# Spreading a recurrence's output projection over three attention stages, in a decoder layer on one core

## The chip, the cores and the metric

The kernel runs on one core of a Trainium2 chip. A core has a matrix engine (TensorE, PE in the profile), a vector engine (DVE), a scalar engine (ACT), a general engine (POOL), and a queue processor that issues transfers (SP); POOL issues transfers too. Each engine takes its instructions in a fixed order and waits on semaphores. The metric is the device time of one execution in microseconds (us), the median of several runs.

## The reference

One layer of a hybrid decoder on 2048 prompt tokens and 8 sample tokens of width 1024. The prompt attends to 256 chosen keys for each query, by softmax over 8 heads; a gated recurrence makes the other half of the mixer's width; one output projection, a residual, RMSNorm and an MLP of width 4096 follow.

```python
aq = rms_norm(aq.reshape(B, L, ATT_HEADS, ATT_HEAD_DIM), q_norm_g)
...
logits = jnp.einsum('btkgd,btskd->btkgs', qg, k_sel).astype(jnp.float32) * ATT_SCALE
logits = jnp.where(valid[:, :, None, None, :], logits, -jnp.inf)
p = jax.nn.softmax(logits, axis=-1).astype(v_sel.dtype)
...
x = x + jnp.concatenate([att, rec.astype(att.dtype)], axis=-1) @ w_out
h2 = rms_norm(x, norm2_g)
x = x + jnp.square(jax.nn.relu(h2 @ w_up)) @ w_down
```

## The kernel before

All products are made in 32-bit precision as three products of a high and a low part (`mm3`, L127 to L129: high by high, high by low, low by high). Rows are tiles of 128 tokens, 16 of the prompt and one with the 8 sample tokens.

The first 1059 us hold the input projection, the indexer, the recurrence and the first choices of keys. From there the rows go through in three groups of tiles (`GROUPS`: 0 to 4, 5 to 10, 11 to 16), each with three stages: attention (`attend_all`), output projection with the second norm (the first loop of `mlp_group`), MLP (its second loop). In attention a unit is one pair of heads of one tile, four units to a tile: `logits` (products `lg`, L993; mask and running maximum on DVE, L995, tile `mx`; the maximum times minus the scale, L1001, tile `nm`; the exponential on ACT, L1002), then `values` (transposes `pt`, L1016; high part on ACT, `ph`; low part on DVE, `pl`; products into `O`, L1031 and L1032, or L1029 in the first five tiles; last two transposes `ob`, L1039). The logits of a unit are issued between the values of the unit before.

The recurrence's half of the output projection does not need the attention: `recurrence_out` makes it for all 16 tiles inside the first group's attention. For a tile it loads the recurrence's rows (`rt`, L929) and the residual (`y`, L931, one buffer), makes four transposes, 24 products of 512 columns into `po`, two additions on DVE (L945), and stores `y` to DRAM (`yD`). `mlp_group` loads `yD` later and adds the attention's half to it (64 additions of 256 columns, L1698).

A tile scheduler sets the order on each engine: it places instructions by priority and by a simulated timeline, in program order for equal priority. Side work is fed in by hand: `along` goes through the steps of a stage, counts the columns that PE processes, and takes one step of a `Track` whenever its rate in columns is reached. Beside the first MLP run the choice of keys for tiles 8 to 11 (`choosing`, 12000 columns a step) and the sample's first part (7000); beside the second MLP run the choice for tiles 12 to 15 (14000) and the sample's second part (9000), which begins with a search by counts over rows of 1025 on DVE (L1333). All start with the output projection of their group.

Weights are loaded in pieces of 512 KB (`load_cols`, `load_row`), rounded to a high part on ACT (L1570); the low part is made on POOL at the first use and reloaded from DRAM afterwards.

## Time and profile before

| | |
|---|---|
| runs before: median (lowest to highest) | 3517.41 us (3514.81 to 3519.64) |
| the profiled execution: its own time | 3515.95 us |
| the profiled execution: span of its instructions | 3514.2 us |
| mean granted TensorE clock, as a share of full speed | 0.977 |
| PE, DVE, ACT, POOL busy, share of the span | 94%, 67%, 63%, 34% |

The busy time of PE counts a product from its start to its modelled end, and products overlap, so that a share of 94% does not mean 94% of what PE could do. Shares over the span hide that the stages differ; the rows further down are taken stage by stage.

### The profile page before, as it was taken

The numbers are of one execution on the slowest core, as the hardware profiler recorded it, in microseconds if no ns is written. First come the engines' busy times: TensorE is split into PE (matmuls) and PEld (weight loads), VectorE is DVE, ScalarE is ACT, GpSimd is POOL, SyncE is SP. The second block draws the span as 40 slices with busy tenths as digits, with TensorE's granted clock in tenths as the row PEclk, the third lists the DMA queues.
The fourth block names the chain that finished last, engine by engine and source line by source line (L and its number), as shares of the span: only waits on it lengthen the run. The fifth ranks groups of instructions, "written<-read, shape, count | busy, mean of one in ns | idle before, by whom it ended". The sixth has DMA issues, their size and how long they took to land. (4 is left out here: it accounts for less than half of the span.)

```text
span 3514.2 us, 56706 instructions
## 1 busy us (share of the span) xinstructions
PE 3315.7 (94%) x20230; PEld 2912.1 (83%) x20230; DVE 2345.8 (67%) x5150; ACT 2202.5 (63%) x4063; POOL 1201.2 (34%) x1460
## 2 busy tenths in 40 slices
PE   8999889999998989989999988999999999999999
PEld 7787788999996778877787778888989788888888
DVE  3577788877684358898795788796384787322323
ACT  5789887777674258858844665765973576333332
POOL 5565776655544035554442101042211000100000
PEclk9999999999999999999999999999999999999999
DMA  6564647464535446555546112334336201444443
GB/s 212 156 177 146 176 144 194 139 165 133 163 104 192 146 133 209 190 170 167 168 148 223 36 59 88 126 100 163 130 127 226 84 25 37 150 144 141 135 136 129
DMA packets 343244, 499.95 MB, mean 142 GB/s; under 512 B 38536, under 2 KB 252144, under 8 KB 341936
## 3 DMA queue, kind: packets, MB, share of 16 engines
q1 hardware_dynamic: 280784, 326.35, 29.4%
q0 software_dynamic: 62176, 169.96, 15.8%
q8 instruction: 159, 2.61, 0.3%
q14 instruction: 125, 1.02, 0.1%
HBM read 374.26 MB, written 121.96 MB: 141 GB/s over the span
## 5 line engine op out<-in xcount | busy, mean ns | idle before, releaser
L528 ACT ACTIVATE jkA<-S,candA 128x1664 int8<-128x1664 f32 (+11 forms) x448 | 586.3, 1310 | 116.8 <-DVE candA L532 101.4
L1748 DVE TENSOR_TENSOR y<-y,dn 128x512 f32<-128x512 f32 x512 | 346.5, 683 | 342.9 <-PE dn L129 339.7
L127 PE MATMUL up<-hh,wh 128*128 128x384 f32 (+2 forms) x1536 | 496.5, 323 | 4.7 <-ACT wh L1570 3.5
L128 PE MATMUL up<-hl,wh 128*128 128x384 f32 (+2 forms) x1536 | 496.2, 323 | 0.0
L129 PE MATMUL up<-hh,wl 128*128 128x384 f32 (+2 forms) x1536 | 491.2, 323 | 4.6 <-DMA wl<-low 3.2
L128 PE MATMUL dn<-dl,uh 128*128 128x512 f32 x1024 | 407.8, 398 | 6.0 <-POOL dl L1574 3.4
L127 PE MATMUL dn<-dh,uh 128*128 128x512 f32 x1024 | 404.5, 399 | 4.8 <-DVE y L1748 4.2
L129 PE MATMUL dn<-dh,ul 128*128 128x512 f32 x1024 | 402.2, 396 | 5.3 <-DVE ul L1724 5.0
L127 PEld LDWEIGHTS up<-hh,wh 128*128 128x128 f32 x1536 | 294.9, 192 | 18.2 <-ACT wh L1570 4.9
L128 PEld LDWEIGHTS up<-hl,wh 128*128 128x128 f32 x1536 | 294.7, 192 | 13.5 <-issue 3.9
L129 PEld LDWEIGHTS up<-hh,wl 128*128 128x128 f32 x1536 | 294.5, 192 | 13.0 <-DMA wl<-low 4.8
L1570 ACT CAST dh<-raw 128x1024 fp32r<-128x1024 f32 x96 | 96.8, 1047 | 284.0 <-PE dn L129 276.7
L129 PEld LDWEIGHTS dn<-dh,ul 128*128 128x128 f32 x1024 | 194.9, 191 | 49.0 <-DVE ul L1724 6.8
L506 DVE SCALAR_TENSOR_TENSOR sl<-ix,iw,sl 128x512 f32<-128x512 f32 (+3 forms) x266 | 180.4, 678 | 78.0 <-ACT ix L502 75.5
L127 PEld LDWEIGHTS dn<-dh,uh 128*128 128x128 f32 x1024 | 193.8, 190 | 42.9 <-DVE y L1748 6.7
L128 PEld LDWEIGHTS dn<-dl,uh 128*128 128x128 f32 x1024 | 195.1, 191 | 38.8 <-POOL dl L1574 4.3
L1724 DVE TENSOR_TENSOR ul<-rl,uh 128x384 fp32r<-128x384 f32 x192 | 114.3, 597 | 157.2 <-ACT uh L1723 155.9
L500 PE MATMUL ix<-IK,iqT 128*128 128x512 f32 (+3 forms) x608 | 187.1, 393 | 28.7 <-DVE sl L506 19.7
L1572 POOL DMA_DIRECT2D dl<-low x64 | 34.9, 545 | 521.9 <-PE dn L129 477.9
L502 ACT ACTIVATE ix<-ix,iw 128x512 f32<-128x512 f32 (+3 forms) x304 | 182.3, 604 | 48.5 <-PE ix L500 45.4
L993 PE MATMUL lg<-KS,aqT 128*128 128x512 f32 (+3 forms) x640 | 195.9, 402 | 14.5 <-DVE mx L995 10.7
L1269 POOL DMA_INDIRECT kg<-in_cache_kidx_dram,pti x128 | 132.3, 1033 | 210.7 <-DVE kt L1271 180.1
(498 smaller groups left out, 9330.6 us busy)
## 6 DMA issues: line engine op xcount, KB each, us to landing
raw<-in_w_up_dram SPq DMA_DIRECT2D x96, 512.0 KB
raw<-in_w_down_dram SPq DMA_DIRECT2D x96, 512.0 KB
wl<-low POOLq DMA_DIRECT2D x72, 512.0 KB
raw<-in_w_in_dram SPq DMA_DIRECT2D x256, 128.0 KB
dl<-low POOLq DMA_DIRECT2D x64, 512.0 KB
wl<-lowp POOLq DMA_DIRECT2D x48, 512.0 KB
low<-wl SPq DMA_DIRECT2D x40, 512.0 KB
low<-dl SPq DMA_DIRECT2D x32, 512.0 KB
```

Of the source, the lines that this page charges most:

```text
L127: nc.tensor.matmul(ps, lh, rh, start=first, stop=False)
L128: nc.tensor.matmul(ps, lh, rl, start=False, stop=False)
L129: nc.tensor.matmul(ps, ll, rh, start=False, stop=last)
L500: nc.tensor.matmul(ps[:, :kn], iqT[:, h], IK[:, i, k0:k0 + kn], start=i == 0, stop=i == 1)
L502: nc.scalar.activation(r[:, :kn], ps[:, :kn], AF.Relu, scale=iw[:, 1, h:h + 1])
L506: nc.vector.scalar_tensor_tensor(sl, r[:, :kn], iw[:, 2, h:h + 1], sl, op0=OP.mult, op1=OP.add)
L528: nc.scalar.activation(jk[:, :n], S[:, :n], AF.Sign, bias=cand.bitcast(F32), scale=-1.0, accum_out=cnt)
L993: nc.tensor.matmul(ps[:, :kn], aqT[:, 2 * u + j], KS[k0 // 512][:, u // 2, i, :kn], start=i == 0, stop=i == 1)
L1269: nc.gpsimd.indirect_dma_start(out=kg_, out_offset=None, in_=kview, in_offset=bass.IndirectOffsetOnAxis(ap=pti[:, b, g, u:u + 1], axis=0))
L1570: nc.scalar.copy(wh, raw)
L1724: nc.vector.tensor_tensor(ul[:, o], rl[:, :cn], uh[:, o].bitcast(F32), op=OP.subtract)
L1748: front["dve"] = nc.vector.tensor_tensor(ys_[t][:, s], ys_[t][:, s], po, op=OP.add)
```

## The change

1. `recurrence_out` now makes tiles 0 to 8 (`FILL[0]`). Tiles 9 to 12 are made by a new function `recurrence_more` beside the second group's attention, tiles 13 to 15 beside the third's (`beside`). It works in quarters of 256 columns: for each quarter the weights are loaded anew, and for each tile a quarter of the residual is loaded (`yq`, two buffers), 12 products of 256 columns are made, and the sum is stored. Its steps have a plain priority. These two attentions have three PSUM buffers for `pt` where they had four.
2. The transposed rows that the MLP reads are two tiles of four blocks for each part (`hh` and `hu`, `hl` and `lu`) where they were one tile of eight; the second one lives only in the MLP.
3. The queries of the prompt are multiplied by minus the scale when they are normalized (`qn`), the mask is positive and the running maximum is a minimum, so that the exponential takes it as it is: `nm` (L1001) is gone.
4. Beside the second MLP the two tracks start 74000 columns late (`HOLD`) and then step faster (13300 and 8500 columns for 14000 and 9000).

```diff
-            return [ph.tile([P, 8, T], F32R, name=x) for x in ("hh", "hl")]
+            return [[ph.tile([P, 4, T], F32R, name=x)] for x in ("hh", "hl")]
...
+        def beside(tiles, rows_, g):
...
+            with tc.tile_pool(name="pf", bufs=1, reuse_waits="tile") as pf, \
+                 tc.tile_pool(name="qf", bufs=1, space=PSUM, reuse_waits="tile") as qf:
+                more = Track(recurrence_more(pf, qf, FILL[g], loads[0]), FRATE[g])
+                more.plain = True
+                along(attend(tiles, rows_, 4, 3, 2), more)
+                more.finish()
...
-            along(attend(GROUPS[1], rows_, 4, 4, 2))
-            choice = choosing(range(LATER, NB), PACE[1])
-            second = Track(part(), PUMP[1])
+            beside(GROUPS[1], rows_, 1)
+            choice = choosing(range(LATER, NB), PACE[1], HOLD[1])
+            second = Track(part(), PUMP[1], HOLD[3])
...
-            along(attend(GROUPS[2], rows_, 4, 4, 2))
+            beside(GROUPS[2], rows_, 2)
...
-            self.steps, self.rate, self.credit, self.done, self.count = steps, rate, 0, False, 0
+            self.steps, self.rate, self.credit, self.done, self.count = steps, rate, -wait, False, 0
...
-    PACE, PUMP = (12000, 14000), (7000, 9000)
+    PACE, PUMP, HOLD = (12000, 13300), (7000, 8500), (0, 74000, 0, 74000)
...
+        qn = pc.tile([P, HD], F32, name="qn")
+        nc.gpsimd.tensor_scalar(qn, qg, -ATT_SCALE, None, op0=OP.mult)
...
-        for t in range(EARLY):
+        for t in FILL[0]:
...
+    FILL, FRATE = (range(0, 9), range(9, 13), range(13, 16)), (0, 16000, 28000)
+
+    def recurrence_more(pf, qf, tiles, load_cols):
+
+        T = len(tiles) * P
+        th = pf.tile([P, 4, T], F32R, name="fh")
+        tl = pf.tile([P, 4, T], F32R, name="fl")
+        for i, t in enumerate(tiles):
+            rt = pf.tile([P, 512], F32, tag="rt", name="rt", bufs=1)
+            nc.sync.dma_start(rt, recD[t * P:(t + 1) * P])
+            turned(qf, "po", 1, rt, P, *([x[:, :, i * P:(i + 1) * P]] for x in (th, tl)))
+            yield
+        for cq in range(4):
+            cs = slice(cq * 256, (cq + 1) * 256)
+            w = load_cols(w_out, cq * 256, (1,))
+            for i, t in enumerate(tiles):
+                y = pf.tile([P, 256], F32, tag="y", name="yq", bufs=2)
+                nc.sync.dma_start(y, xp[t * P:(t + 1) * P, cs])
+                po = qf.tile([P, 512], F32, tag="po", name="po", bufs=1)
+                r = slice(i * P, (i + 1) * P)
+                for k in range(4):
+                    mm3(po[:, :256], th[:, k, r], tl[:, k, r], w[k][0], w[k][1], k == 0, k == 3)
+                nc.vector.tensor_tensor(y, y, po[:, :256], op=OP.add)
+                store(yD[t, :, cs], y)
+                yield
...
-                                                   op0=OP.add, op1=OP.max, accum_out=m2)
+                                                   op0=OP.add, op1=OP.min, accum_out=m2)
...
-                nm = p2.tile([P, 1], F32, tag="nm", name="nm", bufs=4)
-                nc.vector.tensor_scalar(nm, mx, -ATT_SCALE, None, op0=OP.mult)
-                nc.scalar.activation(L[:, :n], L[:, :n], AF.Exp, bias=nm, scale=ATT_SCALE, accum_out=sm[:, j:j + 1])
+                nc.scalar.activation(L[:, :n], L[:, :n], AF.Exp, bias=mx, scale=-1.0, accum_out=sm[:, j:j + 1])
...
-        hh, hl = rows_
+        hh, hl = ([x[0], p3.tile([P, 4, T], F32R, name=name)] for x, name in zip(rows_, ("hu", "lu")))
```

The lines have other numbers in the changed kernel: products of the logits are L1034 there, `pt` L1055, `O` L1070 and L1071, the sums of the output projection L1741, the counts of the sample's search L1372.

On PE nothing moves before row 5070, the start of the first attention. In the second attention, PE before has, from the third unit on:

```order
L1039 MATMUL ob<-ident,ot 128x128 x2
L1016 MATMUL pt<-ident,L 128x128 x12
L1031 MATMUL O<-ph,VS_22346 128x256
L993 MATMUL lg<-KS_22343,aqT 128x512 x2
L1032 MATMUL O<-pl,VS_22346 128x256
```

In the change the same place has groups of 12 products (`fh` and `fl` are the turned recurrence rows) between two `pt` and again between the `O`; this is the first of them:

```order
L1078 MATMUL ob<-ident,ot 128x128 x2
L1055 MATMUL pt<-ident,L 128x128 x8
L1034 MATMUL lg<-KS_21980,aqT 128x384 x2
L127 MATMUL po<-wh,fh 128x256
L128 MATMUL po<-wl,fh 128x256
L129 MATMUL po<-wh,fl 128x256
L127 MATMUL po<-wh,fh 128x256
L128 MATMUL po<-wl,fh 128x256
L129 MATMUL po<-wh,fl 128x256
```

All 16 groups of the second attention stand in its units 3 to 7 of 24 (3, 3, 4, 3, 3 of them), and all 12 groups of the third attention in its units 1 to 4 of 20 (2, 4, 4, 2); `pt` runs of 12 have become 8 and 4. In the first attention the last product of `recurrence_out` stands in unit 13 of 20, where it stood in unit 17.

On SP, in the change, loads and stores of the quarters take turns in the second attention, each load with a wait for an earlier transfer and each store with a wait for DVE (in brackets):

```order
L1015 DMA MB<-mbD 128x1024 [waits DMAHW4_49,DVE_49]
L135 DMA yD<-yq 128x256 [waits DMAHW5_49,DVE_49]
L980 DMA yq<-in_x_prompt_dram 128x256 [waits DMAHW5_49]
L135 DMA yD<-yq 128x256 [waits DMAHW7_49,DVE_49]
L980 DMA yq<-in_x_prompt_dram 128x256 [waits DMAHW7_49,DMAHW0_49]
```

Before, SP has at this place only the masks of the next tiles and nothing between them:

```order
L974 DMA MB<-mbD 128x1024 [waits DMAHW5_49,DVE_49]
L974 DMA MB<-mbD 128x1152 [waits DMAHW6_49,DVE_49]
L974 DMA MB<-mbD 128x1280 [waits DMAHW7_49,DMAHW5_49,DVE_49]
```

On DVE, in the second group's output projection, the order before puts the sample's counts (`jk,cntS`) and the choice's steps between the sums:

```order
L1333 TENSOR_SCALAR jk,cntS<-KH,cs 128x1025
L532 SCALAR_TENSOR_TENSOR candA_25014<-incA_25015,candA_25014 128x1
L1333 TENSOR_SCALAR jk,cntS<-KH,cs 128x1025
L1698 TENSOR_TENSOR y<-y,po 128x256
L1333 TENSOR_SCALAR jk,cntS<-KH,cs 128x1025
L529 TENSOR_SCALAR incA_25025<-cntA_25027 128x1
L532 SCALAR_TENSOR_TENSOR candA_25024<-incA_25025,candA_25024 128x1
L1698 TENSOR_TENSOR y<-y,po 128x256
```

In the change the first 12 sums stand together, and the counts come later:

```order
L1354 SCALAR_TENSOR_TENSOR KH<-sg,X 128x1025
L1741 TENSOR_TENSOR y<-y,po 128x256 x12
L1388 TENSOR_SCALAR cs<-three,cH 128x3
L1741 TENSOR_TENSOR y<-y,po 128x256
L1372 TENSOR_SCALAR jk,cntS<-KH,cs 128x1025 x2
L1741 TENSOR_TENSOR y<-y,po 128x256
```

Of the 24 counts that stand ahead of this stage's last normalized rows before, 9 do so in the change; the other 15 have moved behind the first products of the MLP.

## Rows read from the trace of the kernel before

**Rows 1.** The page's head and busy time of each engine.

```profile
span 3514.2 us, 56706 instructions
PE 3315.7 (94%) x20230; PEld 2912.1 (83%) x20230; DVE 2345.8 (67%) x5150; ACT 2202.5 (63%) x4063; POOL 1201.2 (34%) x1460
```

**Rows 2.** Busy time of each engine in stages; first line names the columns.

```profile
core 0: us, PE busy (x) PEld busy (x) DVE busy (x) ACT busy (x) POOL busy (x), PEclk, DMA share, GB/s
1059.00:1254.00 195.00, 183.60 (x925) 133.98 (x923) 74.79 (x234) 77.96 (x193) 42.70 (x46) 1.00 0.52 175
1896.00:2089.00 193.00, 179.88 (x1130) 144.81 (x1128) 147.94 (x437) 131.42 (x259) 23.87 (x55) 0.99 0.12 37
2089.00:2155.00 66.00, 49.52 (x353) 46.60 (x353) 61.09 (x146) 32.03 (x46) 8.68 (x17) 0.85 0.31 105
2155.00:2735.00 580.00, 567.55 (x3265) 511.29 (x3266) 391.61 (x882) 377.22 (x520) 113.32 (x149) 0.99 0.43 146
2735.00:2977.00 242.00, 228.60 (x1493) 191.04 (x1491) 196.46 (x513) 164.00 (x271) 22.28 (x48) 0.99 0.09 27
2977.00:3030.00 53.00, 45.21 (x359) 43.10 (x358) 26.31 (x49) 17.77 (x32) 13.36 (x20) 0.90 0.52 170
```

**Rows 3.** Line L945's waits of DVE (us, times), and the stores of `yD`.

```profile
  DMA y<-in_x_prompt_dram: 48.5, 12
...
L135 SPq DMA_DIRECT2D yD<-y x16: 319/320/1620, 1101.2 to 1235.6; - x16
```

**Rows 4.** Timeline of the first attention, SP and DVE: start, duration, instruction, wait.

```profile
1112.65 1.29 DVE L945 TENSOR_TENSOR y<-y,po 128x512 f32<-128x512 f32 x2
1114.08 1.62 SPq L135 DMA_DIRECT2D yD<-y  x1
1118.55 0.33 SPq L931 DMA_DIRECT2D y<-in_x_prompt_dram  x1
1122.01 0.69 DVE L945 TENSOR_TENSOR y<-y,po 128x512 f32<-128x512 f32 x1 [2.24 <-DMA y<-in_x_prompt_dram]
1123.38 0.32 SPq L135 DMA_DIRECT2D yD<-y  x1
```

**Rows 5.** Timeline of PE: the first attention's last two units.

```profile
1248.39 0.34 PE L1039 MATMUL ob<-ident,ot 64*128 64x64 f32 x2 [0.46 <-ACT ot L1036]
...
1253.24 0.34 PE L1039 MATMUL ob<-ident,ot 64*128 64x64 f32 x2 [0.46 <-ACT ot L1036]
```

**Rows 6.** Timeline of PE: products of 512 and then of 256 columns.

```profile
1098.15 0.39 PE L127 MATMUL po<-wh,th 128*128 128x512 f32 x1
...
1099.28 0.39 PE L129 MATMUL po<-wh,tl 128*128 128x512 f32 x1
...
2102.11 0.28 PE L127 MATMUL po<-wh,hh 128*128 128x256 f32 x1
...
2103.31 0.28 PE L128 MATMUL po<-wl,hh 128*128 128x256 f32 x1
```

**Rows 7.** Timeline of PE: ends of units 2, 7 (second attention); 1, 4 (third).

```profile
1916.45 0.44 PE L1039 MATMUL ob<-ident,ot 128*128 128x128 f32 x2 [0.30 <-ACT ot L1036]
...
1949.51 0.38 PE L1039 MATMUL ob<-ident,ot 128*128 128x128 f32 x2
...
2756.61 0.44 PE L1039 MATMUL ob<-ident,ot 128*128 128x128 f32 x2
...
2787.59 0.44 PE L1039 MATMUL ob<-ident,ot 128*128 128x128 f32 x2
```

**Rows 8.** DVE's groups in 2089 to 2155: shapes, count, busy us, mean ns, idle.

```profile
L1333 DVE TENSOR_SCALAR_CACHE_REDUCE jk<-KH,cs 128x1025 bf16<-128x1025 int16 x24 | 30.7, 1281 | 0.2
L1698 DVE TENSOR_TENSOR y<-y,po 128x256 f32<-128x256 f32 x24 | 10.0, 416 | 0.5 <-PE po L129 0.5
```

**Rows 9.** Line L1001: minimum, median, maximum ns, first and last start.

```profile
L1001 DVE TENSOR_SCALAR nm<-mx x128: 134/150/155, 1060.4 to 2958.6; 128x1 f32<-128x1 f32 x128
```

**Rows 10.** Transposes of `rt` (L934) on PE: ns, first and last start.

```profile
L934 PE MATMUL tp<-ident,rt x64: 269/272/331, 1089.8 to 1217.5; 128*128 128x128 f32 x64
```

More of the change, by code (lines that the diff above doesn't have):

```diff
@@ L229, in trunk, with choosing @@
         cx.close()
-        def choosing(blocks, rate):
+        def beside(tiles, rows_, g):
[5 more added lines that the diff above has]
+                more.finish()
+        def choosing(blocks, rate, wait):
             px = cx.enter_context(tc.tile_pool(name="px", bufs=1, side="right", reuse_waits="tile"))
-            return Track(choose_all(choose_keys(px), blocks), rate)
+            return Track(choose_all(choose_keys(px), blocks), rate, wait)
         with ExitStack() as ctx_:
@@ L240, in trunk @@
                 recurrence_out(pf, qf)
-            choice = choosing(range(AHEAD, LATER), PACE[0])
-            first = Track(part(), PUMP[0])
+            choice = choosing(range(AHEAD, LATER), PACE[0], HOLD[0])
+            first = Track(part(), PUMP[0], HOLD[2])
             along(mlp(GROUPS[0], rows_), choice, first)
@@ L273, in hymba_kernel, with __init__ @@
     class Track:
-        def __init__(self, steps, rate):
-            self.steps, self.rate, self.credit, self.done, self.count = steps, rate, 0, False, 0
+        plain = False
+        def __init__(self, steps, rate, wait=0):
+            self.steps, self.rate, self.credit, self.done, self.count = steps, rate, -wait, False, 0
         def step(self):
             with ExitStack() as held:
-                for x in front.values():
+                for x in () if self.plain else front.values():
                     held.enter_context(tc.issue_after(x.ins))
-                with tc.high_priority(offset=2000):
+                with tc.high_priority(offset=0 if self.plain else 2000):
                     self.done = next(self.steps, "end") == "end"
@@ L977, in prep @@
                 nc.gpsimd.affine_select(MB[:, b * P:n], MB[:, b * P:n], pattern=[[-1, P]], compare_op=OP.is_ge,
-                                        fill=NEG, base=0, channel_multiplier=1)
+                                        fill=-NEG, base=0, channel_multiplier=1)
             return aqT, MB
@@ L1081, in attention @@
                     c = (b - blocks[0]) * P
-                    turned(q2, "pt", PTB, att, P, *(x[:, :, c:c + P] for x in rows_), 1)
+                    turned(q2, "pt", PTB, att, P, *([x[0][:, :, c:c + P]] for x in rows_))
         return attention
@@ L1577, in parts, with load_cols @@
             return wh, wl
-        def load_cols(w, c0, halves=2):
+        def load_cols(w, c0, halves=range(2)):
             out = []
             src = w[0]
-            for i in range(halves):
+            for i in halves:
                 def fill(x):
@@ L1604, in w_out_parts, with turned @@
     def w_out_parts(tiles):
-        return 1 if tiles[-1] < EARLY else 2
-    def turned(pool, tag, bufs, x, n, hi, lo, parts):
-        for hf in range(parts):
+        return range(1 if tiles[-1] < EARLY else 2)
+    def turned(pool, tag, bufs, x, n, hi, lo):
+        for hf in range(len(hi)):
             ps = pool.tile([P, 512], F32, tag=tag, name="tp", bufs=bufs)
@@ L1627, in mlp_group, with transposed, cols @@
         load_cols, load_row, load_mix = loads
-        def transposed(x, n, hi, lo, parts=2):
-            turned(q3, "dn", DN, x, n, hi, lo, parts)
-        hh, hl = rows_
+        def transposed(x, n, hi, lo):
+            turned(q3, "dn", DN, x, n, hi, lo)
+        hh, hl = ([x[0], p3.tile([P, 4, T], F32R, name=name)] for x, name in zip(rows_, ("hu", "lu")))
+        def cols(x, k, c, n):
+            return x[k // 4][:, k % 4, c:c + n]
         ys_ = {}
@@ L1667, in mlp_group @@
             if t == NB:
-                transposed(load_mix(t)[:n], n, st[:, :, :NS], st[:, :, 32:])
+                transposed(load_mix(t)[:n], n, *([st[:, 4 * i:4 * i + 4, o:o + NS] for i in range(2)] for o in (0, 32)))
         g2 = pw.tile([P, D], F32, tag="io", name="g2", bufs=IO)
@@ L1680, in normalize @@
             nc.vector.scalar_tensor_tensor(hn[:n], y[:n], r[:n, 0:1], g2[:n], op0=OP.mult, op1=OP.mult)
-            transposed(hn[:n], n, hh[:, :, c:c + n], hl[:, :, c:c + n])
+            transposed(hn[:n], n, *([y[:, :, c:c + n] for y in x] for x in (hh, hl)))
         for cq in range(4):
```

14 lines of the change are left out of this document (7 added, 7 removed).

## The prediction

> **What bounds the kernel now.** I read the page's head first: PE is busy in 94% of the span, DVE in 67% [rows 1]. That makes PE the engine to count, but a product counts as busy until its end while the next one has long started: in a run without waits a product of 512 columns starts every 0.226 us (1098.15 to 1099.28, five steps) though each is busy 0.39, one of 256 columns every 0.120 us (2102.11 to 2103.31, ten steps) though each is busy 0.28 [rows 6]. A PE that looks busy may therefore be waiting, and I went on by stages [rows 2]: first attention 195 us, second 193, third 242, second output projection 66, second MLP 580.
>
> In the first attention, DVE waits 48.5 us in 12 waits for the load of `y` [rows 3]. One cycle shows how: additions at 1112.65, store at 1114.08, and only at 1118.55 the next load, because `y` has one buffer and the store must end first; DVE starts again at 1122.01 and stores at 1123.38 [rows 4]. The 16 stores stand 134.4 us apart from first to last, 8.96 us for each of 15 cycles [rows 3]. A tile of 24 products and four transposes needs PE for only 24 x 0.226 + 4 x 0.11 = 5.9 us (0.11 is my estimate for a transpose, which is busy 0.272 [rows 10], less the 0.16 us by which the products' busy time stands over their step). So this attention is paced by the round trip of `y` through DRAM. At its end, with no tile left to fill, a unit takes 4.85 us (1248.39 to 1253.24) [rows 5].
>
> In the second output projection DVE is busy 61.1 of 66 us and PE 49.5 at a granted clock of 0.85 [rows 2]: here DVE is the limit, and 30.7 us of it are the sample's 24 counts [rows 8]. The third output projection, with five tiles and the sample and no side work, takes 53 us with DVE busy 26.3 [rows 2].
>
> **The change part by part.** The profiled execution took 3515.95 us, 1.46 under the median of 3517.41; the sum is made against it.
>
> *First attention, 16 tiles to 9.* The ninth store comes after eight cycles, 1101.2 + 8 x 8.96 = 1172.9. By the order seven units remain behind the last product's unit: three of tile 3 and four of tile 4. Those of tile 4 take 4.85 us; those of tile 3 have four blocks of keys for five, 3.9 us as an estimate: 31 us together. With 1 us for the rest of the thirteenth unit the stage ends near 1205, and before it ended at 1253.24 + 0.34 [rows 5]: **-48 us**, of which I take -47. Bounds: if the round trip were no limit, only PE's 7 x 5.9 = 41 us would go; if the remaining units ran without their wait for `ot` and the like, at about 3.5 us, some 9 us more: -41 to -57.
>
> *Second attention, four tiles.* PE gets 16 groups of 12 products, 16 x 12 x 0.12 = 23 us, and 16 transposes, 1.8 us. All groups stand in units 3 to 7, which took 1916.45 to 1949.51, 33.1 us [rows 7]. From below: PE idles 13.1 us in this stage by its busy time [rows 2], so at best 24.8 - 13.1 = +12 us remain, or less where the tails of products hide more; I put the lower end at +7. From above: each group needs a quarter of the residual loaded and the sum stored. Before, load to addition took 3.46 us (1118.55 to 1122.01), additions 1.37, store to the next load 4.47 (1114.08 to 1118.55), all for 512 KB [rows 4]. With two buffers that is at most (3.46 + 0.42 + 4.47) / 2 = 4.2 us a group (0.42 is the sum of 256 columns [rows 8]), 67 us for 16: +34. For 128 KB it must be less; I take 3.3 us, an estimate two thirds of the way from PE's 1.44 to that bound, since PE and DVE hold their order and both wait for the load: 53 - 33 = **+20**. The four loads of `rt` have one buffer, and each must land between transposes that stand a few products apart: 1.5 us each as an estimate, **+6** (0 to 12). Behind a waiting sum on DVE stand the maxima of the logits and the low parts `pl`, and for these PE waits.
>
> The Trainium skill says otherwise on the size of a transfer (DMA: Bandwidth & Descriptors, Anatomy of one DMA): about 2.0 us of a transfer are fixed, and the bytes cost little. By its fit the 512 KB load takes 3.2 us as an estimate, and the 3.46 us above agree with it [rows 4]. By it a quarter takes 2.3 us each way, a group (2.3 + 0.42 + 2.3) / 2 = 2.5 us, the filled units 40 us, and the sum below comes out near -42 in place of -24, since the third attention then falls to its lower end too.
>
> *Third attention, three tiles.* 12 groups, mostly in units 2 to 4, which took 2756.61 to 2787.59, 31 us [rows 7]. At 3.3 us: 40 - 31 = +9; by PE, 12 x 1.44 + 1.3 of transposes against 13.4 us of idle time in the whole stage [rows 2], from +5; by the upper price 12 x 4.2 - 31 = +19. I take **+10**, and **+4** for three loads of `rt`.
>
> *Weights.* They come again in quarters, eight loads of 512 KB with eight casts on ACT and low parts made once on POOL. ACT is busy 131 of 193 us and POOL 24 in the second attention [rows 2], so these hide; without that cover a late piece costs its load, 3.5 us as for `y` [rows 4], once. 0.
>
> *Width.* 168 products of 512 columns become 336 of 256: 336 x 0.120 - 168 x 0.226 = +2.4 us [rows 6]; it is inside the two terms above. The Trainium skill gives a sustained spacing of 131 ns at 512 columns and 81 at 128 (TensorE: Matmul & The Clock Gate, Back-to-back issue gap). By it, with 98 ns at 256 as an estimate between them, halving would cost 336 x 0.098 - 168 x 0.131 = 11 us and speak against the change; the trace has 226 and 120 ns [rows 6] and disagrees.
>
> *`nm`.* 128 instructions of 0.150 us go [rows 9], 6.0 to 7.2 us of DVE in each attention. Only the second maximum of a unit stands ahead of an exponential that PE waits for: 0.2 us a unit as an estimate (0 to 0.3), 24 + 20 units: **-9**. The first attention ends on PE's work, nothing taken there. The multiplication by `qn` takes the place of one that was there.
>
> *Three `pt` buffers.* No row shows a wait for the fourth; 0 to 0.2 us a unit, 0 to +9. I take **+3**, near the lower end, since the waits that PE shows at a unit's end are for ACT's `ot` [rows 5, 7].
>
> *Second output projection.* 15 of 24 counts leave: 15 x 1.28 = 19.2 us of DVE [rows 8]. DVE's 61.1 becomes 42, the third projection needs 53 with one tile less and the sample [rows 2]; I take 66 to 52, **-14** (-6 to -19). The 19 us go into an MLP in which DVE is busy 392 of 580 us [rows 2]; a tenth of the steps now comes in less time: **+3** (0 to 14).
>
> *Two tiles for each part* moves no work: same casts, same products. Their memory is freed by the attention; the loads of `y` waited for that before as well. 0.
>
> Sum: -47 + 20 + 6 + 10 + 4 - 9 + 3 - 14 + 3 = -24. I take no change in the clock. That is 3492 us in the profile and 3493 as a median.
>
> **The rivals.** *The fill hides.* The loads come early enough, and PE puts the groups into time in which it only drained. Terms at their lower ends: +7, 0, +5, 0: -47 + 12 - 9 + 3 - 14 + 3 = -52, 3465 us. The second attention's +7 means a group in (33 + 7) / 16 = 2.5 us, load and store included. The Trainium skill's fit for a transfer (DMA: Bandwidth & Descriptors, Anatomy of one DMA) points this way. For it: 13 us of idle time in each stage [rows 2] and a DMA share of 0.12 and 0.09. Against: the first attention, where fill never hid from its round trip.
>
> *The gain goes back elsewhere.* The counts only move: MLP gives back all 14, and `pt` costs 9 with the fill as taken: -47 + 40 - 9 + 9 = -7, 3510 us, no change. For it: DVE stays the same in sum. Against: 188 us of DVE idle in that MLP [rows 2].
>
> *The quarters hold DVE (the slower side).* One mechanism: SP issues in order, a load of a quarter stands behind the store before it, that store behind a sum; a late load then stops DVE, as 48.5 us show for `y` [rows 3]. If a group costs the full round trip, as without the second buffer, 8.35 us, 28 groups take 234 us where the units took 64: +170 in place of the +30 taken, 3633 us. It decides from 31 us over the +30, (64 + 30 + 31) / 28 = 4.5 us a group, little over the 4.2 that two buffers give for four times the bytes; at 4.7 us the time is 3531. Against: two buffers, and little other traffic (DMA share 0.12 and 0.09 [rows 2]).
>
> **How the numbers follow.** As taken 0.60; hides 0.18; goes back 0.10; quarters hold DVE 0.12. About 0.2% (7 us) is what a measurement of this kernel can tell from no change: faster is under 3510.4, slower over 3524.4. As taken, with the bounds of its terms (not all at one end), gives 3472 to 3512, 0.58 of it faster and 0.02 the same; hides is all faster; goes back is 0.03 faster, 0.05 the same, 0.02 slower; quarters hold DVE is 0.01 faster, 0.03 the same, 0.08 slower. Faster 0.80, same 0.10, slower 0.10. With a tenth left out on either side the range is 3463 to 3520; the likeliest case's own is 3472 to 3512.
>
> **What would show each step.** Stores of `yD` from `recurrence_out` 8.9 us apart, nine of them, and the first attention near 150 us. Units 3 to 7 of the second attention about 53 us for 33, units 2 to 4 of the third about 41 for 31, with DVE waits named after `yq`; no instruction `nm`; the second output projection near 52 us with nine counts in it; the second MLP within a few us of 580. The prediction is wrong if the first attention does not shrink by 40 us, or if the two later ones grow by over 60 together.

## The result, and the profile after

The changed kernel took 3541.61 us (median of five runs, 3540.62 to 3552.48) where the kernel before, run beside it, took 3519.64. The ratio of the two is 1.0070, with an interval of 1.0055 to 1.0085: it is slower by 25 us (the medians alone are 22 us apart), outside the range, and on the other side of the forecast.

The profiled execution is the slowest of the five (3552.48 us). Its head and its stages (columns as in [rows 2]; the six stages in the order of that group):

```profile
span 3550.8 us, 57005 instructions
PE 3323.0 (94%) x20398; PEld 2925.6 (82%) x20398; DVE 2351.0 (66%) x5036; ACT 2216.8 (62%) x4071; POOL 1199.1 (34%) x1469
...
1062.50:1215.00 152.50, 143.24 (x724) 101.30 (x723) 57.97 (x173) 73.73 (x186) 42.86 (x48) 0.98 0.47 162
...
1861.50:2091.00 229.50, 202.77 (x1338) 172.11 (x1337) 155.00 (x408) 140.56 (x267) 29.87 (x58) 0.97 0.25 78
2091.00:2147.50 56.50, 46.44 (x343) 43.99 (x343) 39.55 (x75) 14.16 (x26) 8.94 (x17) 0.90 0.35 121
2147.50:2735.00 587.50, 571.91 (x3277) 513.18 (x3278) 414.42 (x953) 394.28 (x540) 110.97 (x149) 0.99 0.44 146
2735.00:3012.00 277.00, 251.16 (x1649) 209.93 (x1647) 200.85 (x488) 170.98 (x278) 22.41 (x52) 0.98 0.16 51
3012.00:3064.50 52.50, 44.65 (x354) 42.56 (x353) 26.21 (x49) 17.59 (x32) 9.58 (x20) 0.90 0.50 170
```

Against [rows 2] the first attention gives 42.5 us and the second output projection 9; the second attention takes 36.5, the third 35, the second MLP 7. The other stages add 9 between them. Such a sum can be the difference of one execution from another: the program up to the first attention took 1056 to 1067 us in the profiles of the runs below. The two profiles are 36.5 us apart, the medians 22.

The first attention's additions and its stores of `yD` (name, count, durations, first and last start), which answer to [rows 3]:

```profile
  DMA y<-in_x_prompt_dram: 21.0, 7
...
L135 SPq DMA_DIRECT2D yD<-y x9: 319/320/1038, 1104.4 to 1176.5; - x9
```

Nine stores stand 72.1 us apart, 9.0 us a cycle, as forecast. The third attention's units end here; these PE rows are units 5 and 20:

```profile
2818.09 0.44 PE L1078 MATMUL ob<-ident,ot 128*128 128x128 f32 x2
...
3009.23 0.44 PE L1078 MATMUL ob<-ident,ot 128*128 128x128 f32 x2 [0.46 <-ACT ot L1075]
```

No fill is left between them, and yet they are 191.1 us apart. The same units took 174.2 before:

```profile
2800.19 0.44 PE L1039 MATMUL ob<-ident,ot 128*128 128x128 f32 x2
...
2974.43 0.44 PE L1039 MATMUL ob<-ident,ot 128*128 128x128 f32 x2 [0.46 <-ACT ot L1036]
```

17 us of the loss lie where the prediction expected a small gain.

### The profile page after: what moved, and what is told of

Read it like the earlier page. It is cut to its first block, busy times and chain, and to the rows that moved or that the text cites. A ratio compares the mean times of both kernels' runs of the same rounds, so it can differ in the third digit from the quotient of the medians.

```text
span 3550.8 us, 57005 instructions
## 1 busy us (share of the span) xinstructions
PE 3323.0 (94%) x20398; PEld 2925.6 (82%) x20398; DVE 2351.0 (66%) x5036; ACT 2216.8 (62%) x4071; POOL 1199.1 (34%) x1469
## 3 DMA queue, kind: packets, MB, share of 16 engines
q8 instruction: 160, 2.62, 0.3%
## 5 line engine op out<-in xcount | busy, mean ns | idle before, releaser
L543 ACT ACTIVATE jkA<-S,candA 128x1664 int8<-128x1664 f32 (+12 forms) x448 | 586.2, 1310 | 113.0 <-DVE candA L547 85.6
L127 PE MATMUL up<-hh,wh 128*128 128x384 f32 (+2 forms) x768 | 251.9, 328 | 9.5 <-ACT wh L1609 6.0
L129 PE MATMUL up<-hh,wl 128*128 128x384 f32 (+2 forms) x768 | 250.7, 326 | 1.5 <-POOL wl L1613 0.8
L128 PE MATMUL up<-hl,wh 128*128 128x384 f32 (+2 forms) x768 | 250.5, 326 | 0.0
L129 PE MATMUL up<-hu,wl 128*128 128x384 f32 (+2 forms) x768 | 245.0, 319 | 2.4 <-issue 2.2
L127 PE MATMUL up<-hu,wh 128*128 128x384 f32 (+2 forms) x768 | 245.8, 320 | 1.1 <-issue 1.1
L128 PE MATMUL up<-lu,wh 128*128 128x384 f32 (+2 forms) x768 | 246.3, 321 | 0.4 <-issue 0.4
L127 PEld LDWEIGHTS dn<-dh,uh 128*128 128x128 f32 x1024 | 193.6, 190 | 51.7 <-DVE y L1791 15.4
L1034 PE MATMUL lg<-KS,aqT 128*128 128x512 f32 (+3 forms) x640 | 197.0, 405 | 19.4 <-DVE mx L1036 16.8
```

What stands on the lines that cost most here:

```text
L127: nc.tensor.matmul(ps, lh, rh, start=first, stop=False)
L128: nc.tensor.matmul(ps, lh, rl, start=False, stop=False)
L129: nc.tensor.matmul(ps, ll, rh, start=False, stop=last)
L543: nc.scalar.activation(jk[:, :n], S[:, :n], AF.Sign, bias=cand.bitcast(F32), scale=-1.0, accum_out=cnt)
L1034: nc.tensor.matmul(ps[:, :kn], aqT[:, 2 * u + j], KS[k0 // 512][:, u // 2, i, :kn], start=i == 0, stop=i == 1)
```

## The experiments

One table for all, in us. A stage runs from its first product on PE to the next stage's, in one profile of each run; the ratio is to the kernel before, run beside it, with its interval. The runs were made on several chips, on which the median of the kernel before lay between 3519.64 and 3522.83, so two runs are better compared by their ratios and stages than by their medians.

| run | first att. | second att. | second out-proj. | second MLP | third att. | median | ratio |
|---|---|---|---|---|---|---|---|
| before | 195.3 | 192.9 | 65.8 | 580.2 | 241.9 | 3519.64 | |
| changed | 152.7 | 229.4 | 56.6 | 587.3 | 277.1 | 3541.61 | 1.0070 (1.0055 to 1.0085) |
| e1_pt3 | 197.7 | 201.2 | 67.5 | 580.1 | 253.2 | 3545.94 | 1.0070 (1.0053 to 1.0087) |
| e2_nospread | 195.5 | 201.8 | 56.8 | 587.8 | 247.7 | 3531.71 | 1.0031 (1.0016 to 1.0046) |
| e3_qn | 198.0 | 197.1 | 67.7 | 581.1 | 243.7 | 3522.43 | 1.0001 (0.9992 to 1.0011) |
| e4_y2 | 193.6 | 192.4 | 67.6 | 580.4 | 241.1 | 3521.91 | 0.9998 (0.9989 to 1.0008) |
| e5_tiles | 198.1 | 199.5 | 67.4 | 581.4 | 244.2 | 3538.31 | 1.0042 (1.0025 to 1.0058) |
| e6_hold | 195.1 | 193.6 | 57.6 | 587.8 | 241.5 | 3522.61 | 1.0000 (0.9989 to 1.0011) |
| e7_nospread_pt3 | 194.7 | 205.1 | 56.6 | 585.7 | 261.3 | 3548.67 | 1.0074 (1.0054 to 1.0095) |
| e8_shared | 154.6 | 213.5 | 58.9 | 588.0 | 256.7 | 3517.62 | 0.9983 (0.9971 to 0.9994) |
| e9_ring3 | 155.5 | 225.1 | 58.1 | 588.0 | 270.6 | 3542.91 | 1.0065 (1.0047 to 1.0082) |
| e10_ring_nm | 159.7 | 211.2 | 59.7 | 585.9 | 257.3 | 3519.30 | 0.9991 (0.9981 to 1.0001) |
| e11_ring_nm_nohold | 163.1 | 210.7 | 68.0 | 579.0 | 259.0 | 3526.54 | 1.0007 (0.9994 to 1.0020) |
| e12_ring_nm_late | 161.4 | 208.0 | 59.3 | 587.7 | 255.7 | 3515.74 | 0.9984 (0.9974 to 0.9994) |
| e13_ring_late | 154.0 | 208.0 | 59.5 | 581.6 | 254.3 | 3507.53 | 0.9954 (0.9942 to 0.9966) |
| e14_tiles_late | 200.1 | 199.8 | 67.7 | 579.5 | 244.1 | 3539.38 | 1.0043 (1.0027 to 1.0059) |

**One buffer less, and nothing else** (the kernel before with):

```diff
-            along(attend(GROUPS[1], rows_, 4, 4, 2))
+            along(attend(GROUPS[1], rows_, 4, 3, 2))
```

and the same for `GROUPS[2]`.

> The kernel before with three pt buffers in place of four in the second and third attention, and nothing else. Theory A (the third attention's unfilled units, 191 us in place of 174 in the changed kernel, and the second's, 137 in place of 130, are longer because the transposes have a buffer less): both show here with no fill at all; second attention 193 to about 203, third 242 to about 260, the whole about 25 us slower, 3542 us. Theory B (the negated queries, whose logits, minima and exponentials now depend on each other in another way, made the units longer): both stages stay within 3 us of before and the whole within 5 us of it. Prediction's term: +3 (0 to 9).

Theory A holds: the two attentions grow by 8.3 and 11.3 us, and the whole is 25 us slower. The third attention stays 7 us under the 260 that the theory had, and 5 of the 25 us lie outside these two stages. Who waits for whom in the third attention's last 15 units is read from the group of `ph` on ACT (busy, mean ns, idle time ahead of it and what ended it). In the kernel before:

```profile
L1023 ACT CAST ph<-pt 128x512 fp32r<-128x512 f32 (+1 forms) x113 | 60.2, 576 | 19.0 <-PE O L1031 12.7 <-DVE pl L1024 3.7 <-PE pt L1016 1.6
```

In this run, the same group:

```profile
L1023 ACT CAST ph<-pt 128x512 fp32r<-128x512 f32 (+1 forms) x113 | 60.7, 576 | 25.7 <-PE pt L1016 23.2 <-DVE pl L1024 2.0
```

And in the changed kernel:

```profile
L1062 ACT CAST ph<-pt 128x512 fp32r<-128x512 f32 (+1 forms) x113 | 60.2, 574 | 24.1 <-PE pt L1055 15.1 <-DVE pl L1063 5.1 <-DVE mx L1036 3.6
```

With four buffers the transposes are done when ACT comes to them: ACT waits for `O`, which frees its own output `ph`, and 1.6 us for `pt`. With three it waits 23 and 15 us for `pt`: as these waits read, the transposes no longer run ahead, and each part goes in turn from PE to ACT, DVE and back. PE's products into `O` then wait for `ph` (in all, times, longest), in this run and in the changed kernel:

```profile
PE O L1031 <- ACT ph L1023: 2.5, 3, 1.2
...
PE O L1070 <- ACT ph L1062: 4.2, 8, 0.8
```

Before, no such wait is listed in these units.

**Negated queries alone**, on the kernel before, with the other lines of the change's third part:

```diff
-                nm = p2.tile([P, 1], F32, tag="nm", name="nm", bufs=4)
-                nc.vector.tensor_scalar(nm, mx, -ATT_SCALE, None, op0=OP.mult)
-                nc.scalar.activation(L[:, :n], L[:, :n], AF.Exp, bias=nm, scale=ATT_SCALE, accum_out=sm[:, j:j + 1])
+                nc.scalar.activation(L[:, :n], L[:, :n], AF.Exp, bias=mx, scale=-1.0, accum_out=sm[:, j:j + 1])
```

> The kernel before with only the third part of the change: queries multiplied by minus the scale, positive mask, running minimum, no nm. Theory A: as the prediction had it, the two later attentions together 0 to 9 us shorter, the whole 3508 to 3519. Theory B: the two later attentions together about 24 us longer, the whole near 3540.

The time is the same, and neither theory's stage numbers came: the two attentions are 4.2 and 1.8 us longer. The exponential waits 8.5 us for the running minimum in the third attention's last units, where it waited 4.3 us for `nm`. The tiny instruction is gone, but the wait for the one ahead of it is not.

**All but the spread** (`FILL` 16, 0 and 0 tiles, four buffers):

```diff
-    FILL, FRATE = (range(0, 9), range(9, 13), range(13, 16)), (0, 16000, 28000)
+    FILL, FRATE = (range(0, 16), range(0), range(0)), (0, 16000, 28000)
...
-            beside(GROUPS[1], rows_, 1)
+            along(attend(GROUPS[1], rows_, 4, 4, 2))
```

> The changed kernel without its first part: all 16 tiles in the first attention again, four pt buffers, nothing beside the two later attentions; two tiles for each part, negated queries and the held tracks stay. Theory A (missing buffer): second attention 185 to 193 us, third 235 to 242, second output projection 56 for 66, second MLP +3 to +7; the whole 5 to 15 us faster than before, 3504 to 3514. Theory B (negated queries): third attention 255 to 260, second 200, the whole 10 to 20 us slower than before.

3531.71 us, at the lower end of B's range, but not for B's reason: the queries alone cost nothing, and the third attention is under what B had. Here the second attention's first unit takes 19.0 us for 12.6. DVE's first addition in this stage waits longer than in the kernel before; the rows of the kernel before and of this run are:

```profile
1898.93 0.69 DVE L995 CUSTOM_DVE_ANT_0 L<-lg,MB 128x512 f32<-128x512 f32 x1 [1.60 <-DMA out_dram<-y]
...
1904.73 0.69 DVE L1036 CUSTOM_DVE_ANT_0 L<-lg,MB 128x512 f32<-128x512 f32 x1 [7.18 <-DMA out_dram<-y]
```

In the changed kernel the wait is 6.72 us. That spoke for the two tiles.

**Two tiles alone**, on the kernel before:

```diff
-            return [ph.tile([P, 8, T], F32R, name=x) for x in ("hh", "hl")]
+            return [[ph.tile([P, 4, T], F32R, name=x)] for x in ("hh", "hl")]
...
-        hh, hl = rows_
+        hh, hl = ([x[0], p3.tile([P, 4, T], F32R, name=name)] for x, name in zip(rows_, ("hu", "lu")))
```

> The kernel before with only the second part of the change: the turned rows in two tiles for each part. Theory: the first logits tile of the second attention lies in memory that the last rows of the MLP give back late, so DVE's first mask addition waits about 7 us in place of 1.6; first unit of the second attention 17 to 19 us for 12.6, of the third 22 to 25 for 21.4; the whole 5 to 9 us slower, 3525 to 3530. Rival: the longer first unit came from the queries or the held tracks; then this run stays within 3 us of before. Prediction's term: 0.

DVE's first addition of the second attention in this run:

```profile
1911.84 0.69 DVE L1033 CUSTOM_DVE_ANT_0 L<-lg,MB 128x512 f32<-128x512 f32 x1 [7.41 <-DMA out_dram<-y]
```

The wait is there, 7.41 us until a store of the MLP's last rows ends, and the two attentions are 6.6 and 2.3 us longer. The whole is 15 us slower (interval 9 to 20), more than the 9 that the two stages show. That the logits lie in memory of those last rows is argued from the store that ends the wait; no run shows it by itself.

The clock takes part in this first unit. PE stands still during the wait: in the changed kernel it is busy 2.5 of the stage's first 10 us, and in the second and third 5 us the granted clock was 0.50 (1.2 GHz) and 0.53, where it was 0.81 and 1.00 before. Over the whole first unit it was 0.74 in the changed kernel, 0.82 in this run and 0.86 before.

**Held tracks alone**, on the kernel before:

```diff
-    PACE, PUMP = (12000, 14000), (7000, 9000)
+    PACE, PUMP, HOLD = (12000, 13300), (7000, 8500), (0, 74000, 0, 74000)
```

> The kernel before with only the fourth part of the change: held tracks and faster steps beside the second MLP. Theory from the stages of the changed kernel: second output projection 57 us for 66, second MLP 587 to 588 for 580, together 0 to 3 us less, the whole 3517 to 3521 on a before of 3520. The prediction's terms (-14 and +3): MLP 583, the whole 3509.

The second output projection and the second MLP of this run (columns as in [rows 2]):

```profile
2100.00:2157.50 57.50, 45.31 (x344) 42.71 (x343) 39.58 (x75) 14.36 (x26) 8.96 (x17) 0.90 0.36 125
2157.50:2745.50 588.00, 573.99 (x3277) 516.44 (x3278) 415.10 (x954) 393.82 (x539) 111.33 (x149) 0.98 0.43 144
```

The output projection gains 8.2 us and the MLP gives back 7.6. Nothing is left.

**A second buffer for `y`:**

```diff
-            y = pf.tile([P, D], F32, tag="y", name="y", bufs=1)
+            y = pf.tile([P, D], F32, tag="y", name="y", bufs=2)
```

> The kernel before with two buffers for y in recurrence_out in place of one, and nothing else. If the first attention is paced by the round trip of y through one buffer, its 16 stores come closer than 8.96 us to each other, nearer the 5.9 us that PE needs for a tile, and the stage falls from 195 to 150 to 170 us; the whole 25 to 45 us faster, 3475 to 3495. Rival (the tile's transposes, high and low parts and the units' own waits set the pace, and the load only ends last): the stage stays within 10 us of 195.

The rival holds: 193.6 us for 195.3. The additions on DVE, from the timeline of the first attention:

```profile
1135.69 0.69 DVE L945 TENSOR_TENSOR y<-y,po 128x512 f32<-128x512 f32 x1 [3.30 <-PE po L129]
1141.71 0.69 DVE L945 TENSOR_TENSOR y<-y,po 128x512 f32<-128x512 f32 x1 [2.11 <-PE po L129]
1145.70 0.69 DVE L945 TENSOR_TENSOR y<-y,po 128x512 f32<-128x512 f32 x1 [3.30 <-PE po L129]
1151.72 0.69 DVE L945 TENSOR_TENSOR y<-y,po 128x512 f32<-128x512 f32 x1 [2.11 <-PE po L129]
1155.71 0.69 DVE L945 TENSOR_TENSOR y<-y,po 128x512 f32<-128x512 f32 x1 [3.30 <-PE po L129]
```

The 48.5 us of waits for the load [rows 3] are gone, and DVE now waits for `po` instead (us, times):

```profile
  PE po L129: 66.9, 31
```

A tile and a unit together take 10.0 us, and the stores stand 10.0 us apart where they stood 8.96: the edit moved the fill as well, and its last product now stands in unit 20 of 20, not in unit 17. The load was not the pace; it only ended DVE's waits last. That PE sets the pace instead is read from its busy time, 188 of 194 us in this stage, and from these waits for it.

**The spread's own price**, at three buffers in both kernels (the run without the spread, with 3 for 4 in `attend`):

> The changed kernel with all 16 tiles in the first attention and nothing beside the later ones, but with three pt buffers: what is left of the difference to the changed kernel is the spread itself. If the fill costs PE's time wherever it stands (about 6 us a tile), the first attention is 195 us here for 153, the second 208 to 212 for 229, the third 257 to 261 for 277, and the whole 3547 to 3553, 5 to 10 us slower than the changed kernel. Rival (the fill's loads and stores delay DVE and with it the units after it, and the buffer matters less here than alone): second 202, third 249, the whole near 3532, 10 us faster than the changed kernel.

The first theory holds, with the second attention 3 us shorter than it said. From this run to the changed kernel the first attention falls by 42.0 us and the other two grow by 24.3 and 15.8: together 2 us gained. The 28 groups cost 40.1 us, 1.43 each, and the 12 products of a group take PE 1.44 [rows 6]. Units 3 to 7 of the second attention and 2 to 4 of the third (columns as in [rows 2]), in this run and then in the changed kernel:

```profile
1921.00:1955.00 34.00, 31.42 (x187) 23.64 (x186) 23.03 (x62) 22.32 (x48) 4.87 (x11) 1.00 0.15 49
2766.80:2799.30 32.50, 31.53 (x200) 25.05 (x199) 27.12 (x70) 23.14 (x38) 3.19 (x7) 1.00 0.10 32
...
1889.20:1945.30 56.10, 50.31 (x380) 47.81 (x378) 31.47 (x81) 27.98 (x53) 6.78 (x15) 0.97 0.48 144
2762.70:2806.00 43.30, 41.46 (x313) 38.58 (x311) 28.25 (x69) 23.97 (x40) 5.46 (x11) 1.00 0.57 176
```

PE is nearly as busy with the fill as without it. The fifteen units of the third attention behind the fill settle what the buffer does in this setting. They take 174.2 us before. With four buffers and no spread (e2, first pair) they take 178.1, and with three, in this run (second pair), 191.3:

```profile
2809.58 0.42 PE L1078 MATMUL ob<-ident,ot 128*128 128x128 f32 x2
...
2987.72 0.44 PE L1078 MATMUL ob<-ident,ot 128*128 128x128 f32 x2 [0.46 <-ACT ot L1075]
...
2810.30 0.44 PE L1078 MATMUL ob<-ident,ot 128*128 128x128 f32 x2
...
3001.60 0.44 PE L1078 MATMUL ob<-ident,ot 128*128 128x128 f32 x2 [0.46 <-ACT ot L1075]
```

The changed kernel has 191.1. Of its 17 us there, 13 are the buffer, 4 came with the negated queries (177.8 with them alone), and the fill adds none.

The fill's cycle in the changed kernel, on DVE and SP, in the stretch where it is densest:

```profile
1905.93 0.42 DVE L985 TENSOR_TENSOR yq<-yq,po 128x256 f32<-128x256 f32 x1 [2.66 <-DMA yq<-in_x_prompt_dram]
1906.15 0.33 SPq L980 DMA_DIRECT2D yq<-in_x_prompt_dram  x1
1906.58 0.38 SPq L135 DMA_DIRECT2D yD<-yq  x1
1908.77 0.42 DVE L985 TENSOR_TENSOR yq<-yq,po 128x256 f32<-128x256 f32 x1 [1.05 <-DMA yq<-in_x_prompt_dram]
1909.02 0.33 SPq L980 DMA_DIRECT2D yq<-in_x_prompt_dram  x1
...
1911.55 0.42 DVE L985 TENSOR_TENSOR yq<-yq,po 128x256 f32<-128x256 f32 x1 [0.53 <-DMA yq<-in_x_prompt_dram]
```

Here a group takes 2.8 us, as two buffers would have it: load to addition 2.62, addition 0.42, store to next load 2.44, halved. That the buffers set this pace is read from the rows; no run had a third one. It is not the price of the fill: over all groups the additions stand 3.5 us apart in the second attention and 3.8 in the third, with the units' own work between them, and PE waits for `yq` only 5.8 and 1.5 us in the units shown above. The Trainium skill (DMA: Bandwidth & Descriptors, Anatomy of one DMA) has about 2.0 us fixed and little for the bytes, for transfers that the general engine issues; 2.3 us for 128 KB as an estimate. SP issues these, and their 2.62 and 2.44 us lie 0.3 and 0.1 over it.

**Four buffers, shared with the fill.** The spread's transposes and products take a buffer of the `pt` ring, and their own bank goes back to it:

```diff
-                    turned(qf, "po", 1, rt, P, ...)
+                    turned(qf[0], "pt", 4, rt, P, ...)
...
-                po = qf.tile([P, 512], F32, tag="po", name="po", bufs=1)
+                po = qf[0].tile([P, 512], F32, tag="pt", name="po", bufs=4)
...
-                along(attend(tiles, rows_, 4, 3, 2), more)
+                along(attend(tiles, rows_, 4, 4, 2, ring), more)
```

> The changed kernel with four pt buffers again; the spread tiles' transposes and products take a buffer of the same ring and no bank of their own. If the missing buffer is the loss, the unfilled units take 134 and 178 us for 137 and 191, and the whole is 15 to 22 us faster than the changed kernel, 3520 to 3527. Rival (products of 12 that hold a buffer of the ring stop the units as much as a missing buffer does): within 6 us of the changed kernel, 3536 to 3547.

3517.62 us: 24 us under the changed kernel by the medians, 31 by the ratios, and the two attentions are 36.3 us shorter. That is more than the buffer alone (17 to 20) explains. The fill's products of high parts (name, count, durations, first and last start), in the changed kernel:

```profile
L127 PE MATMUL po<-wh,fh x112: 277/282/416, 1890.5 to 2800.7; 128*128 128x256 f32 x112
```

The same products in this run:

```profile
L127 PE MATMUL po<-wh,fh x112: 277/283/385, 1922.2 to 2965.5; 128*128 128x256 f32 x112
```

With a bank of its own the fill was placed early and packed, up to four groups in a unit. In the shared ring a unit mostly takes one group: over units 7 to 23 of the second attention and 6 to 19 of the third. DVE waits for no load there any more (before that 19.8 us for `yq`), and against the run without spread at four buffers the groups cost 11.7 us for 16 and 9.0 for 12: 0.74 us each, where packed ones cost 1.5 in the second attention and 1.3 in the third.

**The same with a ring of three:**

```diff
-                along(attend(tiles, rows_, 4, 4, 2, ring), more)
+                along(attend(tiles, rows_, 4, 3, 2, ring), more)
```

> The shared ring again, with three buffers in place of four: the fill then stands in the order of its steps, one group to a unit, as with four, and only the number of buffers differs. If both count (a buffer less costs about 3 us in the second and 14 in the third attention; groups that stand one to a unit cost about half of packed ones), second attention 215 to 222 us, third 268 to 275, the whole 3532 to 3540, between the changed kernel and the shared ring of four. Rival 1 (only the packing of the groups mattered): within 4 us of the shared ring of four, 3514 to 3522. Rival 2 (only the count of buffers mattered): as the changed kernel, 3538 to 3546.

The same placement (one group to a unit, in the same units) with three buffers is 25 us slower than with four (+11.6 and +13.9), where theory had 15 to 22; the second attention is over its forecast, and the time is Rival 2's. Its stages are still 4.3 and 6.5 us under the changed kernel's. Of the 36.3 us that the two attentions gain in the shared ring, the buffer then makes 25.5 and the placement 10.8; the whole doesn't show the placement's part (ratios of 1.0065 and 1.0070).

**Putting it together.** The shared ring with `nm` (from the shared ring, the diff of the queries backwards):

> The shared ring of four with the queries, the mask and nm as in the kernel before (parts 1, 2 and 4 of the change). If the negated queries make the unfilled units longer by their order, as the stages of the run with them alone had it (+4 and +2 us), the second attention is 208 to 211 us for 213.5, the third 252 to 256 for 256.7, the whole 3510 to 3515. Rival (the difference was between runs): 3515 to 3520. The prediction's term (-9 for the negated queries): 3524 to 3528.

3519.30, in the range of the rival: the queries are worth nothing in the whole here either. What they cost later they give back in the first attention, where the prediction took none: with nine tiles there it takes 159.7 to 163.1 us in the three runs with `nm` and 152.7 to 155.5 in the four without. A part of this can be the granted clock, which was 0.98, 0.95 and 0.96 in the three and 0.98 to 0.99 in the four; at 0.98 in both, 159.7 stands against the changed kernel's 152.7. To the end of its thirteenth unit it is 116.5 us in the shared ring and 120.4 here, from there to the last unit 36.9 and 38.1, so that most of it arises while there is fill. With 16 tiles no such gain shows (198.0 us for 195.3); why not is open.

With the tracks as before (`HOLD` zero, 14000 and 9000):

> As the run with the shared ring and nm, with the tracks beside the second MLP as in the kernel before (parts 1 and 2 alone). If holding the tracks only moves time, the second output projection is 66 us for 57, the second MLP 580 for 588, and the whole within 4 us of that run. The prediction's terms (-14 and +3): 11 us slower than that run.

The output projection and MLP change as expected, 68.0 and 579.0 us. The whole is 7 us slower than with the held tracks, between the two forecasts (4 and 11). These two stages show 1.4 of it, and the intervals of the two ratios overlap.

The second tiles behind the residual rows, in `mlp_group`:

```diff
-        hh, hl = ([x[0], p3.tile([P, 4, T], F32R, name=name)] for x, name in zip(rows_, ("hu", "lu")))
...
             ys_[t] = y
...
+        hh, hl = ([x[0], p3.tile([P, 4, T], F32R, name=name)] for x, name in zip(rows_, ("hu", "lu")))
```

> As the run with the shared ring and nm, with the second tiles of the turned rows (hu, lu) placed in memory after the MLP's residual rows and not ahead of them. If the second attention's first logits wait for memory under the last stored rows, this place changes the wait: first unit 12 to 14 us for 17 to 19, the whole 4 to 6 us faster. Rival (the wait comes from the size of the tiles or the queue, not their place): first unit unchanged, the whole within 3 us.

The first unit fell from 16.1 to 10.5 us, more than forecast, and the granted clock in it was 1.00 for 0.79. 2.5 us of it went to the units up to the eighth, and the median fell by 3.6, with overlapping intervals.

**Both mends on the changed kernel** (the shared ring of four, `hu` and `lu` late, negated queries, held tracks):

> The changed kernel with two mends: the shared ring of four pt buffers, and hu and lu behind the MLP's residual rows. If the gains add, the first attention stays at 153 to 156 us (negated queries, where the runs with nm had 160 to 163), the second falls from 213.5 to about 209, and the whole is 2 to 5 us under the shared ring alone, 3512 to 3517, 0.1% to 0.3% faster than before. Rival (the wait's end only moves to the next unit): the second attention stays at 212 to 214, the whole 3516 to 3520.

3507.53 us: the gains add, to 0.46% less than before (interval 0.34 to 0.58), more than the 0.1% to 0.3% that was expected. This beats both kernels. Three rows for the three attentions:

```profile
1062.00:1216.00 154.00, 142.01 (x728) 101.07 (x726) 59.76 (x173) 74.35 (x186) 42.68 (x48) 0.99 0.47 160
1864.00:2072.00 208.00, 195.19 (x1338) 166.80 (x1336) 153.11 (x408) 138.14 (x267) 29.92 (x58) 1.00 0.26 83
2713.00:2967.00 254.00, 243.19 (x1647) 206.76 (x1645) 199.02 (x488) 169.99 (x278) 22.43 (x52) 1.00 0.18 56
```

The second attention's PE is busy 195 of 208 us. The second MLP was 4 to 6 us shorter than in the other runs with held tracks (581.6 for 585.7 to 588.0); why was not tried.

**The late place without the spread** (two tiles alone, with the edit of the late place):

> The run with two tiles alone, which was about 15 us slower than before with 6 of them at the second attention's first unit, now with hu and lu behind the residual rows. If their place in memory makes all of it, 3520 to 3526; if it makes only the first unit's wait, 3530 to 3534; if two tiles cost by something else, such as their products, 3536 to 3540.

Without the spread the later place changes nothing: first unit 19.1 us, whole 3539. It is not the place alone that makes the wait, and of the two tiles' 15 us some 6 stay unexplained.

## Why the prediction was wrong

The step that failed first is the term "three `pt` buffers", put at +3 with a bound of +9. It costs 20 us alone (e1) and 17 in the changed kernel's setting (from e2 to e7, 3.3 and 13.6). The argument for it, that no row shows a wait for the fourth buffer, has it backwards: a trace with four buffers can't show the wait that comes when one is missing, and only who runs ahead says what the fourth is worth. The order of PE did say it (runs of 12 transposes became 8 and 4), and ACT's waits did as well (12.7 us for `O`, 1.6 for `pt`).

From the forecast of -24 to the measured +25 are 49 us, and this term makes 14 of them. The rest is in the list: 15 for `nm` (about 7 of which came back in the first attention), 9 for the two tiles, 9 for the second output projection with its MLP, and 4 for the first attention; together 51, as near as single profiles tell. The prediction's own sign of being wrong came too: the two later attentions grew by 71.7 us together, over its 60.

By the prediction's own terms, in the two later attentions and around them:

- **Fill and `rt`, +40 together: 40.1** (from e7 to the changed kernel). The size came by luck, since the mechanism was another. The prediction let the round trip of the quarters set the pace, at 3.3 us a group; the groups cost 1.43 us each, PE's own time, and PE waited 7 us for `yq` in the filled units. These took 33 us more than in e7 for 30 taken, and the first units, which hold `rt` and two of the groups, about 5 for 10. The bound of 4.2 us a group rested on one store to the next load of 4.47 us; in the 15 cycles of the kernel before it is 2.6 to 5.6 us.
- **First attention, -47: -42.6.** The size was near by luck, the mechanism wrong. The round trip of `y` was not its pace (e4), and the bound "only PE's 41 us" was nearest. Of the 42.6, about 7 belong to the missing `nm`; in the three runs with it seven tiles less gave 34 us on average (195.3 to 161.4), 4.8 a tile.
- **`nm`, -9: +6** in the two later attentions and about -7 in the first, together none in the whole (e3, e10).
- **Two tiles, 0: +9** in the two attentions (e5), most of it in a wait that ends with a store of the MLP's last rows. The prediction took it that this wait would stay as it was.
- **Second output projection and MLP, -14 and +3: -9.2 and +7.1**; alone -8.2 and +7.6 (e6). "Goes back elsewhere" was right for this term. In the shorter projection PE is busy 46 of 56.5 us at a granted clock of 0.90 and DVE only 40, so DVE is no longer its limit; the MLP is longer by about what the projection lost.
- **Weights: 0**, not seen apart from the fill. **Clock:** taken as unchanged; it was lower in the second attention's first unit (0.74 for 0.86), which lies within the +9 of the two tiles.

The chain of runs adds up: the two later attentions together take 434.8 us before, 449.5 with all but spread and buffer, 466.4 with the buffer gone, 506.5 with the fill. Put into the sum: -42.6 + 40.1 + 17 + 6 + 9 - 2 is +27, against 25 measured.

None of the rivals is what happened. "The quarters hold DVE" was nearest in kind, since packed groups do wait for their loads (19.8 us on DVE, and PE behind it), but with 3.5 and 3.8 us from one group to the next it is short of its point of 4.5. "The fill hides" holds by half in the shared ring (0.74 us a group for the 1.44 that PE needs), once the groups stand apart.

Open are 6 of the two tiles' 15 us, why the later place ends the wait only beside the spread, and what made the second MLP of the best version shorter. That the negated queries lengthen the later units through the order on DVE is argued from the waits only.

## What to carry to other kernels

A buffer taken out of a ring between engines (buffers that are filled and freed in turn) is priced by which engine runs ahead through it, not by waits in a trace that still has it; the run with only that buffer taken away is the cheapest test of a change that needs its bank. A long wait for a load need not be the pace of a stage when another engine is busy nearly throughout: give the load a buffer and see what the wait turns into. Work moved beside other work costs PE's time where PE has no gap; here it hid best at one piece to a unit, and a bank of its own let the scheduler pack what should stand apart.

## What the hardware showed that was not expected

A load and a store of 128 KB take 2.62 and 2.44 us to the next instruction that waits for them. With four times the bytes a load takes 3.46 us [rows 4], and a store to the next load 2.6 us at the least in the kernel before, so that a transfer in quarters costs far more than a quarter each time.

The program up to the first attention, in which only the sign and scale of the queries and the sign of the mask differ between the runs, took 1056 to 1067 us in one profile each. The granted clock goes along with it: it was 0.98 in this stretch of the shortest (e3) and 0.97 in the longest (e6). A stage of one profile therefore tells a few us at best: the first MLP took 588.5 to 593.5 us in the four kernels whose code for it is the same (before, e1, e4, e6). Small terms have to be read from the same units in several kernels: the last 16 units of the second attention, for example, repeat to 0.1 us in the runs whose code for them is the same (129.9, 129.8, 129.8, 129.9 and 129.9).
